# HGRN level scores of two heads at a time, as 64x64 blocks on both halves of TensorE's columns

## The chip, the core and the metric

The kernel runs on one core of a Trainium2 chip, in one launch. The metric is the device time of that launch in microseconds (us). A core has four computing engines that run their own instruction lists in order and wait for each other by semaphores: TensorE (PE, with its weight loads shown apart as PEld), VectorE (DVE), ScalarE (ACT) and GpSimd (POOL). SyncE (SP) issues most DMAs. TensorE reads SBUF and writes PSUM.

## The reference

One encoder layer on 512 tokens of width 1024. Its token mixer projects the normed input (`xn @ w_in`, 4624 columns), splits the columns into groups, and runs two kinds of recurrent heads over the sequence, forward and backward: four HGRN2 heads and four mLSTM heads of width 128. Cross-attention to 256 memory tokens and a squared-ReLU MLP follow. The change concerns the HGRN2 scan; for one chunk it is

```python
cum = jnp.cumsum(lfc, axis=-2)
o_inter = jnp.einsum('bhtd,bhde->bhte', qc * jnp.exp(cum), state)
diff = cum[:, :, :, None, :] - cum[:, :, None, :, :]
decay = jnp.exp(jnp.where(tril[:, :, None], diff, -jnp.inf))
scores = jnp.einsum('bhtd,bhsd,bhtsd->bhts', qc, kc, decay)
o_intra = jnp.einsum('bhts,bhse->bhte', scores, vc)
```

A token t so sees every earlier token s with a weight that decays, per channel, by the product of the forget gates between them; the backward scan does the same for later tokens, with gates of its own, and the two are summed.

## The kernel before, in words

**Projections.** A weight block of 128x1024 is loaded by SyncE (`st`, L203), split by ScalarE and VectorE into a high part `wh` (L224) and a low remainder `wl` (L225), and multiplied in three matmuls per 128 of depth (`mm3`, L228 to L230), 24 matmuls of 512 columns per block. Three pairs `wh`, `wl` exist, so a block is split up to two blocks ahead. These matmuls fill most of TensorE's time.

**Chains.** The recurrent heads are written as Python generators ("chains"). The projections call `tick()` twice each (once in the middle, once behind), and a tick takes one or more steps of the two foremost chains by turns. The build's scheduler may still move instructions on an engine where others are ready earlier; the order that results is fixed in the program.

**An HGRN head** (`hgrn_chain`, L351) holds the whole sequence of 512 tokens: q, the gates f and the keys k of both directions as [channels, tokens]. It builds the full 512x512 score matrix A without a scan, by levels L = 1, 2, 4, ..., 64: at level L, pairs of neighbouring runs of L tokens are joined. The decayed queries `q2` and keys `k` are kept such that one matmul per window of 128 tokens gives all scores between the two runs of each pair (L379, four matmuls per level, fp32). Then `update` (L419) multiplies the run products into q2, k and f: three VectorE instructions (L429, L432, L436), the last one shorter at every level. `kcomb` (L367) interleaves the two directions' keys for the next level on ScalarE (L369), and `copy_predicated` (L384) takes the entries of this level out of the PSUM tile into the diagonal windows of A under a mask of 128x128 per level. The diagonal itself comes from one more round of four matmuls (L364, copied by L365). Scores between windows follow: distance 128 (L391, L392, copied by L394 and L395), then the two halves of the sequence (L403, L405, copied by L407). At the end A is multiplied with the values (L412, 16 matmuls), the result copied out (L415), and `head_out` (L438) normalises it: four squares with their sums (L444), the root on GpSimd (L170), scaling (L446), transposes on TensorE (L453), the gate (L454) and the split into `yT`.

**Order.** Heads 0 and 1 are two chains that go by turns while `hgrn_gate(0)`, `hgrn_proj(1)`, `qk_proj(0)` and `hgrn_gate(1)` project (L697 to L702). `qk_proj` makes mLSTM queries and keys, whose convolution (`conv_evac`, L586) takes six VectorE instructions per projection (L595, L597 four times, L602). `drain()` takes what is left of the chains; then heads 2 and 3 start (L704), and `mv_proj` takes two steps per tick. After that come the mLSTM heads. `smb()` hands out four PSUM tiles ("sm") in turn for the chains, `mmb()` four others ("mm") for the projections.

Of the kernel before, what the change touches and what calls it, by code (L numbers as in the profile page):

```python
# [45 lines left out]
def _split_order():  # L46
# [11 lines left out]
    seq += d("in", 2560, 2) + d("in", 3072, 2) + d("in", 2304, 2)  # L58
# [21 lines left out]
def trunk(ctx: ExitStack, tc: tile.TileContext, x, mem, wpk, vec, cst, lmask, rmask, rows, out):  # L80
# [41 lines left out]
    lm = sb.tile([P, len(LEVELS) * P], U8, name="lm")  # L122
# [22 lines left out]
    def small_setup():  # L145
# [3 lines left out]
        v.tensor_copy(lm, lmf[:, 0:len(LEVELS) * P])  # L149
# [201 lines left out]
    def hgrn_chain(h, s_):  # L351
        q, f, k = s_["q"], s_["f"], s_["k"]
        q2 = A4()
        v.tensor_tensor(out=q2[:, 0:512], in0=q[:, 0:512], in1=f[:, 512:1024], op=ALU.mult)
        v.tensor_tensor(out=q2[:, 512:1024], in0=q[:, 0:512], in1=f[:, 0:512], op=ALU.mult)
        A = A16()
        Adiag = ap(A, 0, [512 + P, 4], [1, P])
        kc = T2()
        v.tensor_tensor(out=kc[:, 0:512], in0=k[:, 0:512], in1=k[:, 512:1024], op=ALU.add)
        yield  # L360
        ps = smb()
        for w in range(4):
            z = slice(w * P, w * P + P)
            pe.matmul(ps[:, z], lhsT=kc[:, z], rhs=q[:, z], start=True, stop=True)  # L364
        sc.activation(Adiag, ps[:, :].rearrange("p (w t) -> p w t", t=P), AF.Copy)  # L365

        def kcomb(L):  # L367
            t = T2()
            sc.activation(t[:, 0:512].rearrange("p (b e j) -> p b e j", e=2, j=L),  # L369
                          ap(k, 0, [2 * L, 512 // (2 * L)], [512 + L, 2], [1, L]), AF.Copy)  # L370
            return t

        kc = kcomb(1)
        yield
        for li, L in enumerate(LEVELS):
            ps = smb()
            for w in range(4):
                z = slice(w * P, w * P + P)
                pe.matmul(ps[:, z], lhsT=kc[:, z],  # L379
                          rhs=ap(q2, w * P, [2 * L, P // (2 * L)], [512 + L, 2], [1, L]), start=True, stop=True)  # L380
            update(q2, k, f, L)
            if L < 64:
                kc = kcomb(2 * L)
            v.copy_predicated(Adiag, lm[:, li * P:li * P + P].unsqueeze(1).to_broadcast([P, 4, P]),  # L384
                              ps[:, :].rearrange("p (w t) -> p w t", t=P))
            yield

# [299 lines left out]
    def hgrn_start(p):  # L687
        for j in range(2):
            chains.append(hgrn_chain(2 * p + j, hst[2 * p + j]))
# [441 lines left out]
```

## Time and profile before

| | |
|---|---|
| time, median of 3 runs | 871.91 us (871.9 to 872.01) |
| the profiled execution's own time | 872.23 us |
| its span, first to last instruction | 870.5 us |
| TensorE busy | 848.8 us (98%) |
| VectorE, ScalarE busy | 577.4 us (66%), 416.1 us (48%) |
| moved by DMA | 113.58 MB, 130 GB/s over the span |
| granted TensorE clock, mean | 0.995 |

In the profile a group of instructions is one line: source line, engine, operation, output tile, input tiles, shapes, count, then busy time in us, mean duration in ns, and the idle time of the engine ahead of them with what ended it. A matmul with fp32 operands appears as two records, each with a weight load of its own; "128*128 128x128" is the part of the array that holds weights (rows by columns) and then the partitions and elements of the moving operand. Timeline rows give start and length in us from the span's start. Matmuls are pipelined: a record lasts longer than the step to the next one. Tiles are named without numbers: `sm` and `mm` are PSUM tiles, `a` the tiles of f, k and q2, `t` short-lived tiles of 512 columns, `as` the score matrix A, `wh`, `wl` the split weights.

### The profile page before, as it was taken

What the parts mean: (1) busy time and instruction counts of PE and PEld (TensorE: products, weight loads), DVE (VectorE), ACT (ScalarE), POOL (GpSimd) and SP (SyncE); (2) the same over time, 40 slices, a digit from 0 to 9 for tenths busy, and PEclk for the clock granted to TensorE, in tenths of its full rate; (3) what the DMA queues carried; (4) which work ended last, traced back from release to release, by engine and by line L of the source; (5) the groups of instructions that cost most, each with busy time, mean ns of one, the idle gap of its engine ahead of it and who ended that gap; (6) DMA issues with size and microseconds to landing.
All of it is one profiled execution on the core that took longest, in us unless ns stands there. A gap on an engine that the chain in (4) does not pass through costs nothing.

```text
span 870.5 us, 11166 instructions
## 1 busy us (share of the span) xinstructions
PE 848.8 (98%) x4182; PEld 707.3 (81%) x4182; DVE 577.4 (66%) x1011; ACT 416.1 (48%) x759; POOL 67.6 (8%) x114
## 2 busy tenths in 40 slices
PE   7999999999999989999999999999999999999994
PEld 5888888888887887888888887888888888888883
DVE  5558688679447987644554455686667656856675
ACT  5336443363358658444544355553454345435544
POOL 2000000010010000000000200002100310120001
PEclk9999999999999999999999999999999999999998
DMA  7332222312134223452222762239955992698322
GB/s 262 131 109 88 74 70 69 113 61 74 50 122 120 98 74 121 146 146 97 73 73 80 185 170 98 98 104 221 271 154 122 249 281 98 165 286 202 119 52 97
DMA packets 32680, 113.58 MB, mean 130 GB/s; under 512 B 3761, under 2 KB 3889, under 8 KB 32626
## 3 DMA queue, kind: packets, MB, share of 16 engines
q1 hardware_dynamic: 23120, 78.84, 26.4%
q0 software_dynamic: 9216, 33.56, 17.3%
q8 instruction: 33, 0.54, 0.3%
q10 hardware_dynamic: 290, 0.47, 0.2%
q14 instruction: 21, 0.17, 0.1%
HBM read 110.76 MB, written 2.10 MB: 130 GB/s over the span
## 4 chain that ended last, share of the span: by engine, by line
PE 50%; DVE 1%; ACT 0%; POOL 0%; issue 0%; POOLq 0%; ACTq 0%
PE mm L229 10%; PE mm L230 10%; PE mm L228 10%; PE sm L1005 5%; PE sm L1006 5%; PE sm L1007 5%; PE mm L1006 1%; PE mm L1005 1%; PE mm L1007 1%; PE sm L230 1%; PE sm L229 1%; PE sm L228 1%; PE sm L778 0%; PE sm L835 0%; DVE vv L930 0%; ACT t L764 0%
## 5 line engine op out<-in xcount | busy, mean ns | idle before, releaser
L224 ACT ACTIVATE wh<-st 128x1024 fp32r<-128x1024 f32 x133 | 140.8, 1059 | 224.2 <-PE mm L229 114.0
L225 DVE TENSOR_TENSOR wl<-st,wh 128x1024 fp32r<-128x1024 f32 x133 | 162.9, 1225 | 119.5 <-ACT wh L224 115.9
L228 PE MATMUL mm<-xT,wh 128*128 128x512 f32 x544 | 215.7, 397 | 0.0
L229 PE MATMUL mm<-xT,wh 128*128 128x512 f32 x544 | 213.2, 392 | 0.3 <-DVE xT L784 0.3
L230 PE MATMUL mm<-xT,wl 128*128 128x512 f32 x544 | 213.3, 392 | 0.0
L229 PEld LDWEIGHTS mm<-xT,wh 128*128 128x128 f32 x544 | 102.3, 188 | 21.8 <-DVE xT L784 2.0
L230 PEld LDWEIGHTS mm<-xT,wl 128*128 128x128 f32 x544 | 102.2, 188 | 21.8 <-issue 0.7
L228 PEld LDWEIGHTS mm<-xT,wh 128*128 128x128 f32 x544 | 102.3, 188 | 20.6 <-issue 0.5
L899 POOL DMA_DIRECT2D as<-in_wpk x48 | 36.8, 776 | 310.9 <-DVE wl L225 185.1
L963 DVE SCALAR_TENSOR_TENSOR t<-mm,rg 128x512 f32<-128x512 f32 x32 | 22.1, 692 | 55.1 <-PE mm L230 55.0
L230 PE MATMUL mm<-wh,yT 128*128 128x512 f32 x128 | 50.6, 395 | 0.0
L228 PE MATMUL mm<-wh,yT 128*128 128x512 f32 x128 | 50.4, 394 | 0.0
L229 PE MATMUL mm<-wl,yT 128*128 128x512 f32 x128 | 50.1, 391 | 0.0
L1005 PE MATMUL sm<-wh,yT 128*128 128x512 f32 x128 | 49.8, 389 | 0.0
L1006 PE MATMUL sm<-wl,yT 128*128 128x512 f32 x128 | 49.8, 389 | 0.0
L1007 PE MATMUL sm<-wh,yT 128*128 128x512 f32 x128 | 49.8, 389 | 0.0
L224 ACT ACTIVATE wh<-as 128x1024 fp32r<-128x1024 f32 x24 | 25.5, 1061 | 33.6 <-PE sm L1007 24.0
L225 DVE TENSOR_TENSOR wl<-as,wh 128x1024 fp32r<-128x1024 f32 x24 | 29.4, 1226 | 14.2 <-ACT wh L224 14.2
L379 PEld LDWEIGHTS sm<-a,t 128*128 128x128 f32 x224 | 30.1, 191 | 2.3 <-ACT t L369 0.4
L938 DVE TENSOR_TENSOR vv<-vv,sm 128x512 f32<-128x512 f32 x48 | 31.0, 681 | 1.2 <-PE sm L1007 1.2
L369 ACT ACTIVATE t<-a 128x512 f32<-128x512 f32 x28 | 18.4, 672 | 27.3 <-DVE a L432 25.5
L379 PE MATMUL sm<-a,t 128*128 128x128 f32 x224 | 30.9, 285 | 0.0
(265 smaller groups left out, 1523.6 us busy)
## 6 DMA issues: line engine op xcount, KB each, us to landing
st<-in_wpk SPq DMA_DIRECT2D x133, 512.0 KB, 3.3
as<-in_wpk POOLq DMA_DIRECT2D x48, 512.0 KB, 6.6
gate<-in_wpk POOLq DMA_DIRECT2D x16, 512.0 KB, 7.7
as<-in_x SPq DMA_DIRECT2D x4, 512.0 KB, 6.4
vv<-in_x SPq DMA_DIRECT2D x8, 256.0 KB, 4.3
out<-vv SPq DMA_DIRECT2D x7, 256.0 KB, 2.3
a<-in_mem SPq DMA_DIRECT2D x2, 512.0 KB, 3.9
t<-in_rows SPq DMA_DIRECT2D x2, 256.0 KB, 5.9
```

The costliest lines, as they stand in the source:

```text
L224: sc.activation(dst_hi, src, AF.Copy)
L225: v.tensor_tensor(out=dst_lo, in0=src, in1=dst_hi.bitcast(F32), op=ALU.subtract)
L228: pe.matmul(ps, lhsT=ah, rhs=bh, start=first, stop=False)
L229: pe.matmul(ps, lhsT=ah, rhs=bl, start=False, stop=False)
L230: pe.matmul(ps, lhsT=al, rhs=bh, start=False, stop=last)
L379: pe.matmul(ps[:, z], lhsT=kc[:, z], rhs=ap(q2, w * P, [2 * L, P // (2 * L)], [512 + L, 2], [1, L]), start=True, stop=True)
L899: gp.dma_start(out=dst, in_=wpk[idx], **kw)
L938: v.tensor_tensor(out=z, in0=z, in1=ps, op=ALU.add if sign > 0 else ALU.subtract)
L963: v.scalar_tensor_tensor(out=y, in0=ps, scalar=0.0, in1=rrow[:, 0:512], op0=ALU.max, op1=ALU.mult)
L1005: pe.matmul(ps, lhsT=ah, rhs=bh, start=new, stop=False, **fl)
L1006: pe.matmul(ps, lhsT=ah, rhs=bl, start=False, stop=False, **fl)
L1007: pe.matmul(ps, lhsT=al, rhs=bh, start=False, stop=end and k == 1, **fl)
```

## The change

**Two heads are one chain.** `hgrn_pair(p)` takes the place of the two generators: each step works on both heads of the pair.

**Blocks of 64x64.** Below L = 64 all scores of a level lie inside 64x64 blocks on the diagonal. So the matmul of a window of 128 tokens becomes two, each with 64 columns of weights (the keys of one half window) and the 64 queries of the same half; the first writes partitions 0 to 63 of the PSUM tile, the second partitions 64 to 127, that is, they use the lower and the upper half of TensorE's columns by turns. Both heads' blocks, 16 matmuls, fill one PSUM tile of 512 columns. The diagonal round is done likewise.

**Collected compactly.** The copies go into a tile D of 128x512 for both heads (the unused end of the first head's A), so one masked copy per level serves two heads, under a mask of 64 columns per level. At the end four ScalarE copies of 64 partitions (two heads, two halves) put D in its places in A. At L = 64 the blocks lie off the diagonal: they are computed with the other half's queries and copied straight into A by four more such copies. `part` builds their addresses.

**Keys in place.** `kcomb` writes the same tile at every level (`kc`, one per head), where it took the next of five before. The first matmul of a level is made to stand behind both heads' updates in the order ("both heads together"), which adds no semaphore wait of its own.

**Order.** The pair takes two steps per level (`pace`). `qk_proj(0)` moves from ahead of `hgrn_gate(1)` to behind the start of heads 2 and 3, and the four extra ticks there go; the weight blocks are stored in the new order, so the list of loads changes with it. The mask of the levels is made by two copies of 64 partitions at the start.

```diff
-    seq += d("in", 2560, 2) + d("in", 3072, 2) + d("in", 2304, 2)
+    seq += d("in", 2304, 2) + d("in", 2560, 2) + d("in", 3072, 2)
...
+        D = A[0][:, 2048:2560]
+        kc = [A[1][:, 2048:2560], T2()[:, 0:512]]
...
+        def scores(ps, rhs):
+
+            for j in range(2):
+                for w in range(4):
+                    for i in range(2):
+                        z = j * 256 + w * 64
+                        mm = pe.matmul(ps[64 * i:64 * i + 64, z:z + 64], lhsT=kc[j][:, w * P + 64 * i:w * P + 64 * i + 64],
+                                       rhs=rhs(j, w * P, i), start=True, stop=True)
...
         for li, L in enumerate(LEVELS):
             ps = smb()
-            for w in range(4):
-                z = slice(w * P, w * P + P)
-                pe.matmul(ps[:, z], lhsT=kc[:, z],
-                          rhs=ap(q2, w * P, [2 * L, P // (2 * L)], [512 + L, 2], [1, L]), start=True, stop=True)
-            update(q2, k, f, L)
             if L < 64:
-                kc = kcomb(2 * L)
-            v.copy_predicated(Adiag, lm[:, li * P:li * P + P].unsqueeze(1).to_broadcast([P, 4, P]),
-                              ps[:, :].rearrange("p (w t) -> p w t", t=P))
+                scores(ps, lambda j, o, i: ap(q2[j], o + 64 * i, [2 * L, 64 // (2 * L)], [512 + L, 2], [1, L]))
+            else:
+                scores(ps, lambda j, o, i: q2[j][:, o + (1 - i) * 576:o + (1 - i) * 576 + 64])
+            for j in range(2):
+                ready[j] = update(q2[j], k[j], f[j], L)
+                if L < 64:
+                    ready[j].append(kcomb(j, 2 * L))
+            if L < 64:
+                v.copy_predicated(D.rearrange("p (w t) -> p w t", t=64), lm[:, li * 64:li * 64 + 64].unsqueeze(1).to_broadcast([P, 8, 64]),
+                                  ps[:, :].rearrange("p (w t) -> p w t", t=64))
+            else:
+                for j in range(2):
+                    for i in range(2):
+                        sc.activation(part(A[j], 64 * (1 - i), 512 + P, i), part(ps, j * 256, 64, i), AF.Copy)
+            for _ in range(pace[0]):
+                yield
+        for j in range(2):
+            for i in range(2):
+                sc.activation(part(A[j], 64 * i, 512 + P, i), part(D, j * 256, 64, i), AF.Copy)
...
     hgrn_proj(1)
-    list(qk_proj(0))
     hgrn_gate(1)
     drain()
     hgrn_start(1)
-    for _ in range(4):
-        tick()
+    list(qk_proj(0))
```

How the order moves, at three places. First TensorE at level 1 of heads 2 and 3, before: the scores of the two heads, then projections (`a` is q2, `t` the interleaved keys).

```order
L379 MATMUL sm_1535<-a_244_1483,t_251_1501 128x128 x4
L379 MATMUL sm_1546<-a_247_1489,t_253_1509 128x128 x4
L228 MATMUL mm_1515<-wh_1377,xT_85 128x512
L229 MATMUL mm_1515<-wl_1378,xT_85 128x512
L230 MATMUL mm_1515<-wh_1377,xT_85 128x512
```

And in the changed kernel (L232 to L234 are the projection's lines there; `as` holds the first head's keys):

```order
L380 MATMUL sm_1444<-a_199_1369,as_1372 64x64 x8
L380 MATMUL sm_1444<-a_200_1370,t_203_1373 64x64 x8
L232 MATMUL mm_1431<-xT_86,wh_1223 128x512
L233 MATMUL mm_1431<-xT_86,wh_1223 128x512
L234 MATMUL mm_1431<-xT_86,wl_1224 128x512
```

Two times four matmuls of 128x128 into two PSUM tiles became two times eight of 64x64 into one, and the projections beside them are those of `qk_proj(0)` now, with 24 to 36 of them between two levels up to L = 16 and 12 from there on, where there were 12 before.

Second TensorE behind level 64 of heads 2 and 3, before: the scores at distance 128 of one head and of the other, with projections between and behind them.

```order
L392 MATMUL sm_1799<-a_244_1483,a_166_982 128x128
L228 MATMUL mm_1824<-xT_85,wh_1665 128x512
L229 MATMUL mm_1824<-xT_85,wh_1665 128x512
L391 MATMUL sm_1808<-a_247_1489,a_156_923 128x128
L392 MATMUL sm_1808<-a_247_1489,a_156_923 128x128
L391 MATMUL sm_1808<-a_247_1489,a_156_923 128x128
L392 MATMUL sm_1808<-a_247_1489,a_156_923 128x128
L230 MATMUL mm_1824<-xT_85,wl_1666 128x512
L228 MATMUL mm_1824<-xT_85,wh_1665 128x512
```

The same place in the changed kernel (L426, L427 are the scores at distance 128, L439, L441 those of the halves, L450 the product with the values `vv`):

```order
L426 MATMUL sm_1835<-a_200_1370,a_153_1039 128x128
L427 MATMUL sm_1835<-a_200_1370,a_153_1039 128x128
L426 MATMUL sm_1835<-a_200_1370,a_153_1039 128x128
L427 MATMUL sm_1835<-a_200_1370,a_153_1039 128x128
L439 MATMUL sm_1856<-a_199_1369,a_146_976 128x256 x2
L441 MATMUL sm_1860<-a_199_1369,a_146_976 128x256 x2
L439 MATMUL sm_1864<-a_200_1370,a_153_1039 128x256 x2
L441 MATMUL sm_1868<-a_200_1370,a_153_1039 128x256 x2
L450 MATMUL sm_1896<-vv_317,as_1371 128x128
```

There is no projection between these steps any more; the 32 products of both heads follow in one piece, then two projection matmuls, the first head's transposes, 17 projection matmuls and the second's. At the end of heads 0 and 1 the products stand in one piece too, with the first head's transposes right behind, 11 projection matmuls, and the second's.

Third VectorE at level 4 of heads 2 and 3, before: three updates and a masked copy for each head.

```order
L429 TENSOR_TENSOR a_244_1483<-a_244_1483,a_165_981 128x2x64x4
L432 TENSOR_TENSOR a_166_982<-a_166_982,a_165_981 128x2x64x4
L384 COPY_PREDICATED as_1486<-lm,sm_1609 128x4x128
L436 TENSOR_TENSOR a_165_981<-a_165_981 128x128
L429 TENSOR_TENSOR a_247_1489<-a_247_1489,a_155_922 128x2x64x4
L432 TENSOR_TENSOR a_156_923<-a_156_923,a_155_922 128x2x64x4
L384 COPY_PREDICATED as_1492<-lm,sm_1620 128x4x128
L436 TENSOR_TENSOR a_155_922<-a_155_922 128x128
```

In the changed kernel, at level 2 (L470, L473, L477 are the updates, L639 the convolution, L229 the split, L410 the masked copy):

```order
L639 SCALAR_TENSOR_TENSOR t_214_1486<-t_213_1482,vc,t_214_1486 128x512
L473 TENSOR_TENSOR a_146_976<-a_146_976,a_145_975 128x2x128x2
L639 SCALAR_TENSOR_TENSOR t_214_1486<-t_213_1482,vc,t_214_1486 128x512
L477 TENSOR_TENSOR a_145_975<-a_145_975 128x256
L639 SCALAR_TENSOR_TENSOR t_214_1486<-t_213_1482,vc,t_214_1486 128x512
L470 TENSOR_TENSOR a_200_1370<-a_200_1370,a_152_1038 128x2x128x2
L229 TENSOR_TENSOR wl_1565<-st_1499,wh_1564 128x1024
L639 SCALAR_TENSOR_TENSOR t_214_1486<-t_213_1482,vc,t_214_1486 128x512
L473 TENSOR_TENSOR a_153_1039<-a_153_1039,a_152_1038 128x2x128x2
L410 COPY_PREDICATED as_1371<-lm,sm_1514 128x512
```

One masked copy remains for both heads, and the convolutions of mLSTM heads 0 and 1 now stand between the updates.

More of the change, by code (lines that the diff above doesn't have):

```diff
@@ L419, in update @@
+        for g in outs:
+            yield from g
     def update(q2, k, f, L):
@@ L687, in hgrn_start @@
     def hgrn_start(p):
[L688 to L689 removed]
+        chains.append(hgrn_pair(p))
     def mlstm_start(p, gt):
```

116 lines of the change are left out of this document (66 added, 50 removed).

## The prediction, made before the run

> **What bounds the kernel now.** I read the page first: the span, the engines' shares, the slices, the chain that ended last.
>
> ```profile
> span 870.5 us, 11166 instructions
> PE 848.8 (98%) x4182; PEld 707.3 (81%) x4182; DVE 577.4 (66%) x1011; ACT 416.1 (48%) x759; POOL 67.6 (8%) x114
> PE   7999999999999989999999999999999999999994
> DVE  5558688679447987644554455686667656856675
> PEclk9999999999999999999999999999999999999998
> PE 50%; DVE 1%; ACT 0%; POOL 0%; issue 0%; POOLq 0%; ACTq 0%
> ```
>
> TensorE is busy for 98% of the span at a granted clock in the top tenth of every slice but the last, and no other engine has more than 1% of the last chain. So the time is TensorE's work plus the few places where it stands still: 870.5 - 848.8 = 21.7 us. A change to VectorE or ScalarE can only act through such a wait. The profiled execution took 872.23 us, 0.3 above the median of the runs shown (871.91); I sum against 872.23 and take off 0.3 at the end.
>
> Next I asked for windows over the stages that the change touches: the HGRN chains of heads 0 and 1, the stretch between, the chains of heads 2 and 3, and the mLSTM stage after them.
>
> ```profile
> core 0: us, PE busy (x) PEld busy (x) DVE busy (x) ACT busy (x) POOL busy (x), PEclk, DMA share, GB/s
> 85.00:142.00 57.00, 57.00 (x312) 49.52 (x311) 43.39 (x73) 23.70 (x35) 0.14 (x2) 1.00 0.22 74
> 142.00:183.00 41.00, 40.55 (x224) 34.99 (x223) 30.34 (x48) 16.24 (x39) 2.80 (x8) 1.00 0.27 90
> 183.00:219.00 36.00, 36.00 (x219) 31.94 (x218) 35.41 (x62) 15.30 (x23) 0.00 (x0) 1.00 0.21 67
> 262.00:322.00 60.00, 56.29 (x355) 47.71 (x354) 50.36 (x114) 41.28 (x101) 3.60 (x12) 1.00 0.31 94
> ```
>
> TensorE is full in both chain stages. In the second, 183 to 219 us, VectorE is full as well (35.41 of 36.00): there is no slack beside TensorE, and a shorter TensorE block gains only as far as VectorE follows.
>
> **What a block of level scores costs now.** The timeline of TensorE around one level (four matmuls of one head, which the trace shows as eight records, two passes each), and around level 1, whose moving operand is read element by element:
>
> ```profile
> 115.19 0.39 PE L230 MATMUL mm<-xT,wl 128*128 128x512 f32 x1
> 115.42 1.05 PE L379 MATMUL sm<-a,t 128*128 128x128 f32 x8
> 116.23 0.48 PE L228 MATMUL mm<-xT,wh 128*128 128x512 f32 x1
> 116.55 0.39 PE L229 MATMUL mm<-xT,wh 128*128 128x512 f32 x1
> 116.78 0.39 PE L230 MATMUL mm<-xT,wl 128*128 128x512 f32 x1
> ```
>
> ```profile
> 92.36 0.39 PE L230 MATMUL mm<-xT,wl 128*128 128x512 f32 x1
> 92.58 1.49 PE L379 MATMUL sm<-a,t 128*128 128x128 f32 x8
> ...
> 94.15 0.39 PE L229 MATMUL mm<-xT,wh 128*128 128x512 f32 x1
> ```
>
> Projection matmuls start 0.227 us apart (116.55 to 116.78 is 0.23). From the L230 at 115.19 to the L229 at 116.55 are 1.36 us with two such steps in them, so the block has cost 1.36 - 0.45 = 0.91 us, 0.112 to 0.114 per record. Level 1 cost 94.15 - 92.36 - 0.45 = 1.34, 1.48 times as much. The groups give the number of records:
>
> ```profile
> L379 PE MATMUL sm<-a,t 128*128 128x128 f32 x224 | 30.9, 285 | 0.0
> L364 PE MATMUL sm<-t,t 128*128 128x128 f32 x32 | 4.1, 275 | 0.0
> L508 PE MATMUL sm<-tiny,a 128*128 128x32 f32 x10 | 1.2, 267 | 0.0
> ```
>
> 256 records are 32 blocks: 28 of them at 0.90 and the 4 of level 1 at 1.34 are 25.2 + 5.3 = 30.5 us, and all of it lies on the path. This is what the change can win from.
>
> **The change, part by part.** First the blocks. 32 blocks of 8 records become 16 blocks of 32 records (two heads, four windows, two halves, two passes), each with 64 columns of weights and 64 moving columns. The columns streamed are as many as before; what is new is that neighbouring matmuls stand in different halves. Let c be the cost of such a block. If strided reads keep their factor of 1.48, the two blocks of level 1 add 2 x 0.48c, about c, so all come to 17c. No row has a matmul with 64 weight columns, so c is bounded. Above: the L508 group has only 32 moving columns, yet ten records take 1.2 us, as dear as 128 columns; if a record had such a floor whatever its size, c = 32 x 0.112 = 3.58. In proportion: half the columns in weights and stream, 0.057 per record, c = 1.82. Below: the same with two halves working at once, c = 0.91. At its edges a block may also pay for the change of width: a projection matmul lasts 0.39 and the next starts after 0.227, so 0.16 us of its tail lies under its successor; if a block had to wait for this tail on entry and leave its own on exit, c rises by up to 0.33.
>
> I take two halves at once with half of the edges: c = 0.91 + 0.16 = 1.07. The reason is in the rows: 0.39-us matmuls start 0.227 apart, so TensorE already has two in work as long as they don't need the same place, and here every second matmul writes other output partitions with other weight columns. It is a choice, not a reading, and the rivals hold the other values. 17 x 1.07 = 18.2, a saving of 12.3 us.
>
> The Trainium skill has this in TensorEngine Tiling (Array Packing), section Tiling Modes: tiles load weights and multiply in parallel, but a change of tiling mode drains TensorE. The first half is the choice above; the second speaks against the change and is what the second rival prices from rows. No trace here shows either.
>
> Second, the masked copies and updates on VectorE. 28 copies become 12; level 64 and the diagonal go to ScalarE as eight small copies per pair of heads, off the path (ScalarE was busy for 15.3 of 36 us). The update's three instructions per head and level stay. But the convolutions of heads 0 and 1, which stood in the loose stretch from 142 to 183, now stand among the levels of heads 2 and 3. Does VectorE still follow there?
>
> ```profile
> L429 DVE TENSOR_TENSOR a<-a,a 128x512 f32<-128x512 f32 x13 | 9.1, 703 | 0.1
> L384 DVE COPY_PREDICATED as<-lm,sm 128x512 f32<-128x512 uint8 x12 | 9.0, 751 | 0.0
> L225 DVE TENSOR_TENSOR wl<-st,wh 128x1024 fp32r<-128x1024 f32 x4 | 4.9, 1233 | 0.2 <-ACT wh L224 0.2
> L436 DVE TENSOR_TENSOR a<-a 128x512 f32<-128x512 f32 (+5 forms) x12 | 4.9, 408 | 0.0
> ```
>
> ```profile
> L597 DVE SCALAR_TENSOR_TENSOR t<-t,vc,t 128x512 f32<-128x512 f32 x16 | 12.0, 748 | 0.5
> L602 DVE SCALAR_TENSOR_TENSOR yT<-t,t 128x512 f32<-128x512 f32 x4 | 2.8, 690 | 2.3 <-ACT t L599 2.3
> L595 DVE TENSOR_SCALAR t<-t,vc 128x512 f32<-128x512 f32 x4 | 2.2, 541 | 0.0
> ```
>
> ```profile
> 214.59 0.77 DVE L384 COPY_PREDICATED as<-lm,sm 128x512 f32<-128x512 uint8 x1
> 215.21 0.72 DVE L429 TENSOR_TENSOR a<-a,a 128x512 f32<-128x512 f32 x1
> 215.81 0.72 DVE L432 TENSOR_TENSOR a<-a,a 128x512 f32<-128x512 f32 x1
> ```
>
> In the new order, between the scores of level 1 and those of level 64 of heads 2 and 3, VectorE has 22 long updates (0.70), 11 short ones (0.41), 5 masked copies (0.75), 6 splits (1.23), and of the convolution 14 + 3 + 4 (0.75, 0.54, 0.69): 15.4 + 4.5 + 3.8 + 7.4 + 10.5 + 1.6 + 2.8 = 46.0 us of durations. In the last fence the starts are 0.62 and 0.60 apart at lengths of 0.77 and 0.72, so dense work takes 0.83 of its durations: 38 us. TensorE has 149 projection matmuls and six blocks there: 33.8 + 6 x 1.07 = 40.2. VectorE is covered by 2 us in 40, and would set the pace only with c under (38 - 33.8) / 6 = 0.7. In the first stage there are 24 projection matmuls and a block per level (5.4 + 1.07) against 4.4 us of updates and copy, one split (1.23) and at most two evacuations (1.5), 7.1 x 0.83 = 5.9: covered too.
>
> Third, the waits that the new order makes. Both heads' output blocks now stand back to back, and the transposes of the first head right behind. What lies between a head's output block and its transposes (copy out, four squares with their sums, a power on GpSimd, the scaling), and how that wait looks today:
>
> ```profile
> L412 PE MATMUL sm<-vv,as 128*128 128x128 f32 x128 | 14.9, 275 | 0.0
> ```
>
> ```profile
> L444 ACT ACTIVATE t<-t 128x128 f32<-128x128 f32 x8 | 2.4, 300 | 0.0
> L444 ACT ACTIVATION_READ_ACCUMULATOR t<-t 128x1 f32 x8 | 1.5, 190 | 0.0
> L415 ACT ACTIVATE t<-sm 128x512 f32<-128x512 f32 x2 | 1.2, 598 | 1.6 <-DVE yT L602 0.8 <-PE sm L412 0.8
> L446 DVE TENSOR_TENSOR t<-t,tiny 128x512 f32<-128x512 f32 x2 | 1.4, 694 | 2.0 <-POOL tiny L170 2.0
> ```
>
> ```profile
> 176.59 1.02 POOL L170 TENSOR_TENSOR tiny<-tiny,misc 128x4 f32<-128x4 f32 x1 [12.02 <-DVE tiny L168]
> 182.55 0.63 PE L453 MATMUL sm<-cs,t 128*128 128x128 f32 x4 [0.45 <-DVE t L446]
> ```
>
> 0.60 + 4 x 0.49 + 1.02 + 0.69 = 4.3 us. The second head's block covers 14.9 / 4 = 3.7 of it: TensorE waits 0.6. Before the second head's transposes stand the first transposes (four, 0.11 each) and 11 projection matmuls (2.5): 0.8 more after that wait. Today 0.45 is lost there, so heads 0 and 1 lose 1.0 more. Behind the chain of heads 2 and 3 the same sum with two projection matmuls more gives 0.2, and the updates of level 64, three long ones in a row on VectorE before the second head's next block, 0.2. Queued behind each of these waits are the projections of the gates, and nothing of theirs can pass. Together +1.4 us; nothing hides it.
>
> Fourth, the order of the weights: the same blocks in another sequence, the SyncE queue issues them in it, and TensorE is fed as before. The mLSTM stage keeps its instructions, but stands otherwise against the splits; the 3.7 us that TensorE idles there (60.00 - 56.29) may shrink or double, so I count 0 with 3 us either way. The mask's two smaller copies at the start cost nothing: TensorE is then in its first projection.
>
> The sum: -12.3 + 1.4 = -10.9; 872.23 - 10.9 = 861.3, less 0.3: 861.
>
> **The rivals.** *The halves take turns, and nothing is lost at the edges.* For it: one weight load follows another in every row, and 64 columns are half of 128. c = 1.82, 17c = 30.9, +0.4 + 1.4 = +1.8: 873.7. By the Trainium skill (TensorE: Matmul & The Clock Gate, section LDWEIGHTS) a load's time goes by its columns, an estimate of 53 ns for 64; that the 32-wide group costs what a 128-wide one does agrees, since its loads have 128 columns.
>
> *The array empties whenever the width changes, and the halves take turns.* The slower case by one mechanism: a block is entered from and left to 128-wide projection matmuls, 16 times each, at 0.16 us a change. c = 1.82 + 0.33 = 2.15, 17c = 36.5, +6.0 + 1.4 = +7.4: 879.3. It is slower from c = 1.71 on (17 x 1.71 + 1.4 = 30.5). For it: the 0.16 us under each successor; against it: the present blocks lose nothing at their edges (8 x 0.112 is 0.90 of their 0.91), though there the width doesn't change.
>
> *A small record has a floor.* 0.112 each as in the L508 group: c = 3.58, +30.4 + 1.4 = +31.8: 904. Against it: those records have 128 weight columns, and only if the number of records and not their columns sets the pace does it hold.
>
> *The change doesn't do what it says:* VectorE sets the pace of heads 2 and 3. By the sum above that needs c under 0.7, or work that comes in bunches; even three waits of 1 us there keep the time inside my range.
>
> **How the numbers follow.** Forecast (both halves at once, c from 0.91 to 1.24): 0.48; alone it spans 855 (-15.0 + 1.4 - 3) to 867 (-9.4 + 1.4 + 3). Turns without edges: 0.14. Turns with edges: 0.22. Floor: 0.16. Differences under 0.2%, 1.7 us, can't be told from none. The forecast is faster over all its span. Of the 0.14 for turns without edges (+1.8, give or take 3) I give 0.01 to faster, 0.05 to the same and 0.08 to slower; the other two are slower. That makes 0.49 faster, 0.05 the same, 0.46 slower. From 856 to 880 lie the forecast and both cases of turns, 0.84; the floor is left out.
>
> **What would show it.** Right: the group of the level scores has 512 records, and in the timeline a block moves the second projection matmul behind it by about 1.1 us (level 1: 1.6); TensorE's busy time falls by some 12 us; waits of 0.6 and 0.8 stand ahead of the head transposes between 170 and 190 us; no wait on VectorE ahead of the scores of heads 2 and 3 exceeds 1 us. Wrong: 1.8 or more per block in place of 1.1; a step of 0.1 us or more between the first score record and the projection ahead of it beyond 0.227; waits at the scores of heads 2 and 3; or idle time of over 7 us in the mLSTM stage.

## The result, and the profile after

| | before | after |
|---|---|---|
| time, median of 4 runs each, taken together | 871.9 us (871.72 to 872.01) | 861.64 us (861.55 to 861.96) |
| ratio to before, 95% interval | | 0.9883 (0.9866 to 0.99) |
| span of the profiled execution | 870.5 us | 859.8 us |
| TensorE busy | 848.8 us | 839.1 us |

The changed kernel is faster by 10.3 us; 861 was forecast. The top of its page:

```profile
span 859.8 us, 11677 instructions
PE 839.1 (98%) x4438; PEld 692.3 (81%) x4438; DVE 566.8 (66%) x996; ACT 422.8 (49%) x773; POOL 67.4 (8%) x114
PE   7999999999999999999999999999999999999994
DVE  5558874699437977654555446676667656756675
```

TensorE stands still for 859.8 - 839.1 = 20.7 us, against 21.7 before, and its work has fallen by 9.7. So the gain is shorter work on the bounding engine, as forecast. The windows that answer to those of before, in order: the levels of heads 0 and 1, what comes behind them, the levels of heads 2 and 3, and the first 60 us of the mLSTM stage. The columns are PE, PEld, DVE, ACT and POOL busy, then clock, DMA share and GB/s.

```profile
82.30:139.30 57.00, 57.00 (x469) 46.53 (x469) 43.90 (x74) 30.13 (x48) 0.00 (x0) 1.00 0.23 75
139.30:160.30 21.00, 19.55 (x124) 17.27 (x123) 9.49 (x16) 8.73 (x27) 2.17 (x4) 1.00 0.30 101
160.30:213.00 52.70, 52.70 (x446) 42.59 (x445) 49.66 (x84) 25.45 (x41) 0.40 (x6) 1.00 0.23 76
248.40:308.40 60.00, 59.50 (x364) 50.45 (x363) 48.91 (x111) 42.02 (x101) 2.22 (x8) 1.00 0.25 84
```

TensorE is full in both stretches of levels, VectorE nearly so in the second (49.66 of 52.70). The mLSTM window now has 0.50 us of idle TensorE where the window of before had 3.71. The stretch behind heads 0 and 1 has 1.45 us of it.

Now one block of level scores in the timeline of the changed kernel, 32 records between projection matmuls, and below it the block of level 1:

```profile
86.08 0.39 PE L234 MATMUL mm<-xT,wl 128*128 128x512 f32 x1
86.40 0.88 PE L380 MATMUL sm<-a,as 128*64 128x64 f32 x16
87.11 0.84 PE L380 MATMUL sm<-a,t 128*64 128x64 f32 x16
87.88 0.50 PE L232 MATMUL mm<-xT,wh 128*128 128x512 f32 x1
88.21 0.40 PE L233 MATMUL mm<-xT,wh 128*128 128x512 f32 x1
...
100.05 0.39 PE L234 MATMUL mm<-xT,wl 128*128 128x512 f32 x1
100.37 0.69 PE L380 MATMUL sm<-a,as 128*64 128x64 f32 x16
100.88 0.64 PE L380 MATMUL sm<-a,t 128*64 128x64 f32 x16
101.45 0.50 PE L232 MATMUL mm<-xT,wh 128*128 128x512 f32 x1
101.78 0.39 PE L233 MATMUL mm<-xT,wh 128*128 128x512 f32 x1
```

(The first five rows are level 1, the last five another level.) From the L234 at 100.05 to the second projection behind the block at 101.78 are 1.73 us, with two projection steps (0.227 each) in them: the block costs 1.28. Level 1, by the same count, costs 88.21 - 86.08 - 0.45 = 1.68. Sixteen records that last 0.22 to 0.27 us each begin and end within 0.69 us. By their starts in the trace they come in twos, 6 to 7 ns apart, one in each half, and two such twos lie 58 ns apart. The step from the projection to the first record is 0.32 in place of 0.227, and the first projection behind the block lasts 0.50 in place of 0.39: the block loses at its edges.

The waits ahead of the head transposes of heads 0 and 1, in the timeline:

```profile
155.30 0.63 PE L495 MATMUL sm<-cs,t 128*128 128x128 f32 x4 [0.55 <-DVE t L488]
159.36 0.63 PE L495 MATMUL sm<-cs,t 128*128 128x128 f32 x4 [0.91 <-DVE t L488]
```

The forecast was 0.6 and 0.8. By the starts of TensorE's records they cost 0.71 and 1.07 us, since a record lasts longer than the step to the next one, and the rows count the wait from its end.

To see where the rest went I took the starts of TensorE's records out of the traces and cut them into five stretches: up to the first block; from there to the end of head 1's transposes; to the end of head 3's; to the last mLSTM head's transposes; the rest. The projections stand in other stretches than before, so 0.227 us for each projection matmul of 512 columns is taken off; in the last stretch it is taken off for every matmul of 512 columns, and half of it for one of 256. What remains, in us:

| stretch | before | after | wide blocks | order alone | old place | one step more |
|---|---|---|---|---|---|---|
| to the first block | 22.7 | 22.5 | 22.2 | 22.5 | 23.0 | 22.4 |
| heads 0, 1 | 29.6 | 25.8 | 30.4 | 30.7 | 25.5 | 24.1 |
| heads 2, 3 | 29.2 | 25.7 | 30.7 | 31.8 | 24.4 | 24.5 |
| mLSTM | 66.6 | 63.1 | 63.1 | 63.3 | 63.1 | 63.1 |
| rest | 25.1 | 25.3 | 25.0 | 25.0 | 25.0 | 25.0 |

(The last four columns are experiments, below.) The first stretch is not touched by the edits and still differs by up to 0.8 between profiles: so much of a difference of one profile says nothing.

By the same count of steps as above, the level blocks are 31.1 us before and 21.8 after (-4.9 in heads 0 and 1, -4.5 in heads 2 and 3). Each pair of heads gives back 1.0 to 1.1 in waits, and the mLSTM stage adds a gain of 3.4 that the forecast had put at zero.

### The profile page after: what moved, and what is told of

The parts are those of the page before. It is cut to its first block, busy times and chain, and to the rows that moved or that the text cites. A ratio compares the mean times of both kernels' runs of the same rounds, so it can differ in the third digit from the quotient of the medians.

```text
span 859.8 us, 11677 instructions
## 1 busy us (share of the span) xinstructions
PE 839.1 (98%) x4438; PEld 692.3 (81%) x4438; DVE 566.8 (66%) x996; ACT 422.8 (49%) x773; POOL 67.4 (8%) x114
## 4 chain that ended last, share of the span: by engine, by line
PE 72%; issue 21%; DVE 3%; POOL 1%; DMA 1%; ACT 1%; POOLq 0%; ACTq 0%; DVEq 0%
PE mm L233 15%; PE mm L232 15%; PE mm L234 15%; PE sm L1045 5%; PE sm L1046 5%; PE sm L1047 5%; PE sm L682 2%; PE sm L667 2%; PE sm L380 1%; POOL tiny L174 1%; PE mm L1046 1%; PE mm L1045 1%; PE mm L1047 1%; PE sm L450 1%; DVE wl L229 1%
## 5 line engine op out<-in xcount | busy, mean ns | idle before, releaser
L229 DVE TENSOR_TENSOR wl<-st,wh 128x1024 fp32r<-128x1024 f32 x133 | 162.8, 1224 | 116.0 <-ACT wh L228 110.9
L232 PE MATMUL mm<-xT,wh 128*128 128x512 f32 x544 | 215.6, 397 | 0.0
L234 PE MATMUL mm<-xT,wl 128*128 128x512 f32 x544 | 212.5, 391 | 0.0
L232 PEld LDWEIGHTS mm<-xT,wh 128*128 128x128 f32 x544 | 102.2, 188 | 22.2 <-issue 0.7
L234 PEld LDWEIGHTS mm<-xT,wl 128*128 128x128 f32 x544 | 102.1, 188 | 21.4 <-issue 0.2
L234 PE MATMUL mm<-wh,yT 128*128 128x512 f32 x128 | 50.6, 395 | 0.0
L232 PE MATMUL mm<-wh,yT 128*128 128x512 f32 x128 | 50.4, 394 | 0.0
L228 ACT ACTIVATE wh<-as 128x1024 fp32r<-128x1024 f32 x24 | 25.5, 1062 | 33.3 <-PE sm L1047 23.7
L229 DVE TENSOR_TENSOR wl<-as,wh 128x1024 fp32r<-128x1024 f32 x24 | 29.4, 1225 | 13.9 <-ACT wh L228 13.9
L174 POOL TENSOR_TENSOR tiny<-tiny,misc 128x1 f32<-128x1 f32 (+1 forms) x18 | 14.2, 788 | 299.0 <-DVE tiny L172 299.0
L228 ACT ACTIVATE yT<-t 128x512 fp32r<-128x512 f32 x32 | 19.8, 629 | 17.0 <-DVE t L1020 16.5
L1045 PEld LDWEIGHTS sm<-wh,yT 128*128 128x128 f32 x128 | 24.0, 188 | 5.0
```

Source lines behind the costliest of these rows:

```text
L174: gp.tensor_tensor(out=r, in0=ms, in1=nh.to_broadcast([P, w]), op=ALU.pow)
L228: sc.activation(dst_hi, src, AF.Copy)
L229: v.tensor_tensor(out=dst_lo, in0=src, in1=dst_hi.bitcast(F32), op=ALU.subtract)
L232: pe.matmul(ps, lhsT=ah, rhs=bh, start=first, stop=False)
L234: pe.matmul(ps, lhsT=al, rhs=bh, start=False, stop=last)
L1045: pe.matmul(ps, lhsT=ah, rhs=bh, start=new, stop=False, **fl)
```

## The experiments

The theory was that two halves work at once where neighbouring matmuls stand in different halves (0.93 us for 32 records), that a block loses 0.35 at its edges, that the blocks carry the gain in the HGRN stages, and that the new order does no more than bring the 3 us in the mLSTM stage and cost the waits. Rivals: the number of columns alone, the order, or the masked copies carry the gain. Unless said otherwise each kernel is the changed one with one edit, and times are medians beside runs of the kernel before on the same chip.

**Both copies of the work, the same edges.**

```diff
-            for j in range(2):
+            for j in (0, 1, 0, 1):
                 for w in range(4):
                     for i in range(2):
```

> Every matmul of the level scores is issued twice (64 records per block instead of 32, the second writing the same values); the number of blocks, and so of entries and exits, stays 16. In the changed kernel a block costs 1.28 us. Theory (0.93 for the body and 0.35 for the edges of a block): the extra 32 records cost 0.93 each time, 1.4 at the level read by single elements, so 16 x 0.93 + 0.5 = +15.4 us: 877. Rival (nothing is lost at the edges, a record costs 0.040 us): +16 x 1.28 + 0.4 = +20.9: 882.5. Work on VectorE, which is near its limit in the stage of heads 2 and 3, gets more cover in both.

Measured: 877.32 us, ratio 1.0063 (1.005 to 1.0077). One block of it in the timeline:

```profile
102.97 0.39 PE L234 MATMUL mm<-xT,wl 128*128 128x512 f32 x1
103.29 0.69 PE L380 MATMUL sm<-a,as 128*64 128x64 f32 x16
103.80 0.64 PE L380 MATMUL sm<-a,t 128*64 128x64 f32 x16
104.27 0.64 PE L380 MATMUL sm<-a,as 128*64 128x64 f32 x16
104.74 0.64 PE L380 MATMUL sm<-a,t 128*64 128x64 f32 x16
105.30 0.50 PE L232 MATMUL mm<-xT,wh 128*128 128x512 f32 x1
105.64 0.39 PE L233 MATMUL mm<-xT,wh 128*128 128x512 f32 x1
```

64 records cost 105.64 - 102.97 - 0.45 = 2.22, so the second 32 cost 0.93 and the edges 1.28 - 0.93 = 0.35. The theory's 877 is met; the rival's 882.5 is not.

**The two heads' blocks apart.** Every level's block is cut into one per head, with a step of projections between:

```diff
+            for h_ in (0, 1):
...
+                    scores(ps, lambda j, o, i: ap(q2[j], ...), (h_,))
...
+                if h_ == 0:
+                    yield
...
-            for _ in range(pace[0]):
+            for _ in range(pace[0] - 1):
                 yield
```

> The two heads' eight matmuls of a level (16 records each) stand as two blocks with projection matmuls between, where the changed kernel has one block of 32 records; in the stage of heads 2 and 3 four or five levels still come together, so there are about 10 more entries and exits. Theory (0.35 us is lost per block at its edges): +3.5 us: 865. Rival (a block's price goes by its records): 861.6, within 0.2%.

Measured: 865.01 us, ratio 0.9925 (0.9912 to 0.9937), 3.4 more than the changed kernel. Its trace has 26 blocks in place of 16, since the diagonals, which the edit leaves whole, and four levels of heads 2 and 3 still stand in one block each; ten more at 0.35 are 3.5 us. A block of 16 records:

```profile
100.64 0.39 PE L234 MATMUL mm<-xT,wl 128*128 128x512 f32 x1
100.96 0.69 PE L380 MATMUL sm<-a,as 128*64 128x64 f32 x16
101.58 0.50 PE L232 MATMUL mm<-xT,wh 128*128 128x512 f32 x1
101.92 0.39 PE L233 MATMUL mm<-xT,wh 128*128 128x512 f32 x1
```

It costs 101.92 - 100.64 - 0.45 = 0.82: half a body (0.47) and whole edges (0.35). This is the same price from the other side. That the change joins two heads in one block is therefore worth something by itself, about 0.35 us per block saved.

**Four matmuls of one half in a row.** Only the order inside a block changes:

```diff
             for j in range(2):
-                for w in range(4):
-                    for i in range(2):
+                for i in range(2):
+                    for w in range(4):
```

> The four matmuls of a window row that use the same half of the columns now stand in a row, instead of alternating between the halves; instructions, sizes and order of everything else are those of the changed kernel (861.6 us). Theory (both halves work at once only where neighbouring matmuls stand in different halves): the body of a block doubles from 0.93 to 1.8 us, 16 blocks, so +14 us: 876, and the 32 records of a block start about 57 ns apart in place of pairs 7 ns apart. Rival (the gain comes from fewer columns per matmul, in whatever order): 861.6, within 0.2%.

Measured: 867.41 us, ratio 0.9948 (0.9933 to 0.9963). Neither: the loss is 5.8 us, where the theory had 14 and the rival none. A block cost 1.67 in place of 1.28. So the order matters, but it needn't be neighbours. In the timeline of one block the tile names tell the heads apart (`as` the first head's weights, `t` the second's):

```profile
101.73 0.79 PE L380 MATMUL sm<-a,as 128*64 128x64 f32 x13
102.30 0.27 PE L380 MATMUL sm<-a,t 128*64 128x64 f32 x1
102.36 0.22 PE L380 MATMUL sm<-a,as 128*64 128x64 f32 x1
102.41 0.22 PE L380 MATMUL sm<-a,t 128*64 128x64 f32 x1
102.41 0.22 PE L380 MATMUL sm<-a,as 128*64 128x64 f32 x1
102.47 0.22 PE L380 MATMUL sm<-a,t 128*64 128x64 f32 x1
102.47 0.22 PE L380 MATMUL sm<-a,as 128*64 128x64 f32 x1
```

The first `t` record, which uses the other half than the `as` records in front of it, starts while three of those are still to start. That gave a new theory: a record may overtake up to three that wait for the other half. Two kernels test it, with longer and with shorter runs of one half.

**All of one half first.**

```diff
-            for j in range(2):
-                for w in range(4):
-                    for i in range(2):
+            for i in range(2):
+                for j in range(2):
+                    for w in range(4):
```

> The changed kernel (861.6 us) with all 16 records of one half of the columns ahead of the 16 of the other in each block; nothing else moves. Theory (the other half starts as soon as no more than three records of the first still wait ahead of it, as the runs of eight in the kernel of four matmuls in a row showed, and its first record then costs 0.05 us more): 27 steps of 0.058 and two switches make a body of 1.66 in place of 0.93, so +0.73 a block, 16 blocks, level 1 a little more: 873.5. First rival (whatever stands in one half in a row costs what runs of eight cost): 867.4. Second rival (no overlap at all): a body of 1.9, 877.

Measured: 874.8 us, ratio 1.0038 (1.0024 to 1.0052). The changed kernel's block of 1.28 became 2.03, +0.75 where 0.73 was forecast; the 1.3 us over the forecast are about what four blocks of heads 2 and 3 lost, in each of which one projection matmul had been put: such a block costs 2.37 with the projection's step taken off, 0.34 more than a whole one, which is one more entry and exit. The point is seen in the middle of a block:

```profile
102.58 0.68 PE L380 MATMUL sm<-a,as 128*64 128x64 f32 x8
103.09 0.46 PE L380 MATMUL sm<-a,t 128*64 128x64 f32 x5
103.33 0.27 PE L380 MATMUL sm<-a,as 128*64 128x64 f32 x1
103.39 0.22 PE L380 MATMUL sm<-a,t 128*64 128x64 f32 x1
103.44 0.22 PE L380 MATMUL sm<-a,as 128*64 128x64 f32 x1
103.44 0.22 PE L380 MATMUL sm<-a,t 128*64 128x64 f32 x1
103.50 0.22 PE L380 MATMUL sm<-a,as 128*64 128x64 f32 x1
103.50 0.22 PE L380 MATMUL sm<-a,t 128*64 128x64 f32 x1
```

In program order 8 `as` and 8 `t` of one half come first, then 8 `as` of the other. The `as` at 103.33 starts after five `t`, and three `t` of the first half start behind it. Here 8 records take 0.68 us, as long as 16 in the changed kernel (0.69).

**Two matmuls of one half in a row.**

```diff
-                for w in range(4):
-                    for i in range(2):
+                for n in range(8):
+                    for w, i in ((n // 4 * 2 + n % 2, n // 2 % 2),):
```

> The changed kernel with two matmuls (four records) of one half ahead of two of the other, all through a block. Theory (up to three records may wait for their half while a later one of the other half starts): the body stays at 0.93 to 1.0 us, 861.6 to 862.8. Rival (only neighbours in different halves overlap fully): half of the loss of four matmuls in a row or more, 864.5 or more.

Measured: 862.12 us, ratio 0.989 (0.9876 to 0.9903). A block cost 1.33: nearly all the overlap is kept with four records of one half in a row. Both kernels bear the new theory out.

**Pairs of heads and new order, but wide blocks.** Cut to its core:

```diff
-                    for i in range(2):
-                        mm = pe.matmul(ps[64 * i:64 * i + 64, z:z + 64], lhsT=kc[j][:, w * P + 64 * i:w * P + 64 * i + 64], ...
+                    mm = pe.matmul(ps[j][:, z], lhsT=kc[j][:, z], rhs=rhs(j, w * P), start=True, stop=True)
...
-                v.copy_predicated(D.rearrange("p (w t) -> p w t", t=64), ...
+            for j in range(2):
+                v.copy_predicated(Ad[j], lm[:, li * P:li * P + P].unsqueeze(1).to_broadcast([P, 4, P]), ...
```

> Pair of heads as one chain in the new order, but the level scores as 128x128 blocks on the whole array, and one masked copy per head and level, as in the kernel before. Theory (the narrow blocks carry the gain, 31.1 us against 21.8): 861.6 + 9.3 = 870.9, with TensorE's busy time up by about as much. Rival (the new order and the fewer masked copies carry it): about 863 to 865.

Measured: 870.69 us, ratio 0.9987 (0.9978 to 0.9996), 9.05 more than the changed kernel. Its TensorE is busy for 847.8 us, 8.7 more. In the table above it differs from the changed kernel by 4.6 and 5.0 in the two HGRN stretches, and elsewhere by 0.3 at most. This kernel has two masked copies per level as well, but its blocks alone account for the loss: they sum to 31.1 us against 21.8. So the narrow blocks carry what those stretches won. A wide block of both heads costs 1.79 here (from the projection at 101.93 us to the second one behind the block at 104.17). Fewer columns per matmul are therefore not enough: the narrow block with all of one half first, at 2.03, is dearer than the wide one.

**The order alone, on the kernel before.**

```diff
-    seq += d("in", 2560, 2) + d("in", 3072, 2) + d("in", 2304, 2)
+    seq += d("in", 2304, 2) + d("in", 2560, 2) + d("in", 3072, 2)
...
-    list(qk_proj(0))
     hgrn_gate(1)
     drain()
     hgrn_start(1)
-    for _ in range(4):
-        tick()
+    list(qk_proj(0))
```

> The kernel before (871.9 us) with the new place of the query and key projections and the new order of weights, and without the four steps before the mv projections: chains of single heads, 128x128 blocks, and masked copies as before. Theory (order and pairing carry only the gain of about 3 us in the mLSTM stage, and cost up to 2 us of waits at the head transposes): 869 to 871. Rival (the order carries most of the gain): 862 to 864.

Measured: 872.6 us, ratio 1.0011 (1.0002 to 1.0019). The rival falls, but the theory's sum is off by 1.6 as well: by the table the mLSTM stage won 3.3, but the two HGRN stretches lost 1.1 and 2.6, where 2 at most was forecast. In its trace the mLSTM window, which begins at 259.3, shows the gain of that stage:

```profile
259.30:319.30 60.00, 59.51 (x363) 50.40 (x362) 48.83 (x111) 41.79 (x101) 2.08 (x8) 1.00 0.30 92
```

and its list of waits where part of that gain was lost again:

```profile
PE sm L403 <- DVE a L425: 1.7, 1, 1.7
PE sm L453 <- DVE t L446: 1.1, 2, 0.8
PE sm L453 <- DVE tiny L168: 1.0, 1, 1.0
```

The first of these is a wait behind the levels of heads 2 and 3 on an update of VectorE, ahead of which a weight split of 1.23 us stands at 224.21. That VectorE comes late to it because of the convolutions, which now stand among those levels beside 14 masked copies, is likely but not shown.

**One masked copy per head.**

```diff
-                v.copy_predicated(D.rearrange("p (w t) -> p w t", t=64), ...to_broadcast([P, 8, 64]), ...
+                for j in range(2):
+                    z = slice(j * 256, j * 256 + 256)
+                    v.copy_predicated(D[:, z].rearrange("p (w t) -> p w t", t=64), ...to_broadcast([P, 4, 64]), ...
```

> The changed kernel with two masked copies of 256 columns per level, one for each head, in place of one of 512. Theory (VectorE's work lies beside TensorE's): 861.6 to 862.5. Rival (the masked copy stands on the path between the levels): +12 to 20 times 0.2 us, 864 or more, with waits at the scores.

Measured: 863.53 us, ratio 0.9906 (0.9893 to 0.992), 1.9 more than the changed kernel, between the two forecasts. VectorE's busy time rose by 0.6 us only. No wait stands at the scores, but one behind the last level of heads 2 and 3, in the timeline:

```profile
214.42 1.23 DVE L229 TENSOR_TENSOR wl<-st,wh 128x1024 fp32r<-128x1024 f32 x1 [0.37 <-ACT wh L228]
215.56 0.42 DVE L468 TENSOR_TENSOR a<-a,a 128x256 f32<-128x256 f32 x1
216.03 1.13 PE L441 MATMUL sm<-a,a 128*128 128x256 f32 x4 [1.42 <-DVE a L468]
```

A weight split has come ahead of the update for which TensorE waits, and six projection matmuls fewer stand in the stretch. In the changed kernel VectorE was busy for 17.75 of the 18 us from 195 to 213, so it probably had little to spare there. Whether the extra copies or the order that the build made of them cost the 1.9 is not told apart.

**The queries and keys at their old place.**

```diff
-    seq += d("in", 2304, 2) + d("in", 2560, 2) + d("in", 3072, 2)
+    seq += d("in", 2560, 2) + d("in", 3072, 2) + d("in", 2304, 2)
...
+    list(qk_proj(0))
     hgrn_gate(1)
     drain()
     hgrn_start(1)
-    list(qk_proj(0))
+    for _ in range(4):
+        tick()
```

> The changed kernel with the query and key projections, the order of weights and the four steps back where they stood before. In its order 12 projection matmuls stand between the output blocks and the head transposes of heads 0 and 1, but the levels of heads 2 and 3 stand only 7 to 16 projection matmuls apart. Theory (the blocks carry the gain wherever they stand; the waits at the transposes of heads 0 and 1, 1.6 us, go; VectorE may fall behind at the levels of heads 2 and 3): 860 to 863. Rival (the new place is needed, since VectorE cannot follow the levels): 866 or more, with waits at the scores of heads 2 and 3.

Measured: 859.85 us, ratio 0.9864 (0.985 to 0.9877), faster than the changed kernel by 1.8. The new place is not needed, and the mLSTM stage keeps its gain (63.1 in the table). But the waits ahead of the transposes of heads 0 and 1 did not go as I had said: one of 1.3 us took the place of two.

```profile
163.27 0.63 ACT L641 ACTIVATE t<-t 128x512 f32<-128x512 f32 x1 [4.66 <-DVE t L639]
...
163.96 0.60 ACT L453 ACTIVATE t<-sm 128x512 f32<-128x512 f32 x1
...
167.36 0.69 DVE L488 TENSOR_TENSOR t<-t,tiny 128x512 f32<-128x512 f32 x1 [1.13 <-POOL tiny L174]
...
168.20 0.63 PE L495 MATMUL sm<-cs,t 128*128 128x128 f32 x4 [1.28 <-ACT t L633]
```

The second head's output block was done at 160.73, but its copy (L453) stands on ScalarE behind an activation of the convolution (L641) that waits 4.66 us for VectorE. The gain came from heads 2 and 3 instead (24.4 against 25.7).

**Half of them at the old place.** The queries ahead of the gates, the keys behind the start of heads 2 and 3:

```diff
+    qk = qk_proj(0)
+    next(qk)
+    next(qk)
     hgrn_gate(1)
     drain()
     hgrn_start(1)
-    list(qk_proj(0))
+    list(qk)
```

> The changed kernel with the queries' half of the first query and key projection put back ahead of the gates of heads 2 and 3, the keys' half left behind the start of the second pair; the weights' order follows it. In its order 12 projection matmuls stand between the output blocks of heads 0 and 1 and their transposes. Theory (the two waits ahead of those transposes, 0.71 and 1.07 us by start to start, are lost time and go): 860.0, give or take 0.5. Rival (what is saved there comes back as a wait on VectorE at the levels of heads 2 and 3, which have 12 projection matmuls less beside them): 861.6 or more.

Measured: 861.04 us, ratio 0.9876 (0.9861 to 0.9891): 0.6 less than the changed kernel where 1.6 was forecast, which the timing can't tell from none. One wait of 1.1 us ahead of the transposes of heads 0 and 1 stayed, and one of 0.9 us on an update came up behind the levels of heads 2 and 3. By the count of starts the stretch of heads 0 and 1 falls from 25.8 to 25.3 and that of heads 2 and 3 rises from 25.7 to 26.2: what was saved came back there, as the rival had it.

**One step more between the transposes,** on top of the kernel with the old place:

```diff
-        for g in outs:
+        for j, g in enumerate(outs):
+            if j == 1:
+                yield
             yield from g
```

> The kernel with the query and key projections back at their old place (859.85 us) and one more step, of 12 projection matmuls, between the first and the second head's transposes of a pair. Theory (the 1.4 us that TensorE waits ahead of the second head's transposes of heads 0 and 1, where ScalarE's copy of that head's output stands behind a convolution, is lost time): 858.4. Rival (the convolution and the evacuations move along, and the wait turns up at another place): 859.8.

Measured: 858.07 us, ratio 0.9843 (0.9829 to 0.9856). The wait of 1.3 us is gone from its list, the stretch of heads 0 and 1 falls from 25.5 to 24.1, and nothing turns up in another. This kernel is faster than both the one before (by 13.6 us) and the changed one, whose interval lies above its own.

**One block less,** on top of that: the diagonal and level 1 as one block, with level 1's weights made ahead.

```diff
-        for j in range(2):
-            ready[j] = [kcomb(j, 1)]
-        yield
...
+            if L == 1:
+                scores(ps, lambda j, o, i: ap(q2[j], o + 64 * i, [2, 32], [513, 2], [1, 1]), [a[:, 0:512] for a in A])
```

> The kernel with a step between (expected at 858.4 us) and the diagonal's matmuls and those of level 1 as one block of 64 records, for which level 1's weights are made ahead, so that 14 blocks remain of 16 with the same records. Theory (0.35 us at the edges of a block): 0.7 us less, 857.7, unless VectorE or ScalarE is late where the levels of heads 2 and 3 now stand closer to what follows. Rival (no price at the edges): 858.4.

Measured: 857.76 us, ratio 0.9841 (0.9828 to 0.9855): 0.3 less, which the timing can't tell from none. In the trace the joined block of heads 0 and 1 costs 2.62, where the two cost 1.28 + 1.68 = 2.96: the 0.34 is there. In heads 2 and 3 it is given back, as a later block was broken by a projection matmul.

## Why the prediction was right, point by point

**TensorE bounds, and the blocks are what can be won.** Right: the blocks fell by 9.3 us where the whole fell by 10.3, and undoing them (wide blocks) loses 9.05.

**Both halves at once, c = 1.07.** The mechanism was right and its body as chosen: 0.93 for 32 records against 0.91. "Half of the edges" (0.16) was the mis-sized term: the edges are 0.35, as large as the upper bound given there (0.33). c is 1.28 and the saving 9.3 in place of 12.3. The rows of the prediction bounded the edges but gave no reason for the half; the bound would have been the better value. The Trainium skill says in TensorEngine Tiling (Array Packing), section Tiling Modes, that tiles multiply in parallel and that a change of tiling mode drains TensorE. The runs agree with both as far as they go: records of the two halves start 6 to 7 ns apart, and a block bears 0.35 us that does not grow with its records.

**Level 1 by a factor of 1.48.** Its body costs 1.68 - 0.35 = 1.33, 1.43 times the 0.93 of the others: right. The edges don't grow with it: in the kernel that does the work twice, its block costs 3.02, which is 1.34 more for the second 32 records.

**VectorE covered by 2 us in heads 2 and 3.** Right for this kernel: no wait stood at the scores, and the longest break inside a block was 0.14 us. But the margin may be thinner than the sum made it: one masked copy per head, and the order alone on the kernel before, each brought a wait on VectorE behind those levels.

**The waits that the order makes, +1.4.** For heads 0 and 1 the rows say 0.55 and 0.91 where 0.6 and 0.8 were forecast; the stretch lost 1.1, with 1.0 forecast. For heads 2 and 3 it was 1.0 in place of 0.4. The sum is 2.1.

**The mLSTM stage, 0 with 3 either way.** It won 3.4, just beyond the 3 allowed, and so repaired the two terms above. The windows of the waits show what went. Before:

```profile
PE sm L453 <- DVE t L446: 1.7, 2, 1.1
PE mm L228 <- DVE tiny L647: 1.6, 1, 1.6
```

After, in the window of the same length, only this one is left:

```profile
PE sm L495 <- ACT t L694: 0.4, 1, 0.4
```

The order alone brings the gain to the kernel before (66.6 to 63.3), without pairs or narrow blocks. It stays with wide blocks, and it stays with the old place of the queries and keys too, where pairs and narrow blocks remain. So the new place is enough for it, and so is the rest of the change without it. Which instruction's place in the stage does it stays open.

So -9.3 + 2.1 - 3.4 = -10.6 stands against a forecast of -10.9: the total was met this closely because a gain that the sum had put at nothing made up for a saving that was forecast too large. That part of the agreement is luck; with edges of 0.35 and nothing else changed, the prediction's own sum would have come to about 864.

**The rivals.** Turns of the halves would have shown as records 57 ns apart; they show only where the program has long runs of one half. A floor of 0.112 per record falls with 0.029. A loss at the change to narrow blocks and back, half of the second rival, is real, and 0.35 is close to its 0.33; whether the array empties there, no row shows.

**The signs it named.** The group has its 512 records, no wait on VectorE stood ahead of the scores of heads 2 and 3, and the step ahead of a block's first record grew by 0.09, just under the 0.1 that would have spoken against it. A block costs 1.28 where 1.1 was named, and TensorE's busy time fell by 9.7 where some 12 was. The two waits of heads 0 and 1 stand at 155 and 159 us and not between 170 and 190, as the queries and keys are now projected behind them.

## What to carry to other kernels

Work that uses half of TensorE's columns paid here where the two halves alternate within a few instructions (1.28 to 1.33 us a block against 1.79 for the wide one), and each block of it bore a fixed price for entry and exit (0.35): join small blocks rather than place them one by one. Where a bounding engine is full, take a fixed loss that the trace can only bound at its upper bound, and count the stages that are only reordered as a term of their own, with experiments that change the order alone. Ahead of a transpose or any step that waits for a chain over three engines, see what stands in front of that chain on each queue: a copy behind another chain's activation cost 1.4 us here, and one more step of independent work took it back.

## What the runs showed of the hardware that was not expected

**Matmuls of the two halves start out of program order.** An engine was said above to run its list in order; here that does not hold to the letter. With all records of one half first, records of the other started while three of the first had not yet (the rows at 103.33 to 103.50 above), and the times agree: 867.4 for runs of eight records, 874.8 for sixteen, 862.1 for four. The Trainium skill has it otherwise in TensorE: Matmul & The Clock Gate, section The mechanism, where matmuls of packed tiles start strictly in program order; for the two column halves of these fp32 matmuls the measurement decides.

**A switch costs a little even so.** A record of the half that had been idle lasts 0.27 us in place of 0.22, and the next one of its half starts some 0.05 later than the 58 ns that otherwise lie between two of one half.
